# MLP up products and attention input projections as seven block products instead of eight

## The chip, the cores and the metric

The kernel runs on one core of one Trainium2 chip. The metric is the device time of one execution in microseconds (us). TensorE is called PE (PEld its weight loads), VectorE DVE, ScalarE ACT, GpSimd POOL, SyncE SP; SP issues most of the DMAs.

## The reference

An encoder trunk of two layers over 1024 tokens of width 1024, in fp32. Each layer is `h = h + mixer(rmsnorm(h) * g)` and then `h = h + square(relu(rmsnorm(h) * g @ w1)) @ w2`, with `w1` 1024x4096 and `w2` 4096x1024. The mixer of layer 0 is a retention with four heads (input projection 1024x6144, output 2048x1024), that of layer 1 a chunked attention with sixteen heads (input projection `h @ w_in`, 1024x3072 for q, k and v; output 1024x1024). A last RMSNorm follows.

## The kernel before

All activations are kept feature-major: `h[m]` holds 128 features of all 1024 tokens. An fp32 product is made of three matmuls on reduced-precision parts: each operand is split into `hi` (a cast, on ACT) and `lo` (source minus `hi`, on DVE or POOL), and `mm3` (L162 to L164) adds hi·hi, lo·hi and hi·lo in PSUM. Each matmul has 128 rows of contraction, 128 output features and 512 tokens (a half, `hf`).

An up product (`proj_up`, `up_group`) takes 128 columns of `w1`, loads them (`wraw`, 512 KB, on SP), splits them (`whi`, `wlo`), and does 8 blocks x 3 = 24 matmuls for each half. The operands `hhi`, `hlo` are made with the gain `g` in `Norm.block`, which `down` calls as soon as a block of `h` is final, so during the last products of the stage before; the scale per token, `rB`, comes from `Norm.finish` behind the first products. In `mlp` four such blocks give 512 features of the hidden layer; relu and scale (DVE, L324), square (ACT) and a split (`uh`, `ul`) leave them in SBUF, and `down` at once multiplies them with 512 rows of `w2` and adds into `h` (DVE, L280). So up and down alternate eight times per MLP, 192 matmuls each. `qk_proj` does the q and k blocks of the attention in the same way and writes them to memory, `proj_tok` makes v token-major. The attention core then loads q and k (`qh`, `kk`), the bias (`bt`) and v (`vst`) per head; the last `qk_proj` is placed behind the loads of the first heads.

Each engine executes its queue in order. The order of the queues comes from a scheduler over the program order; pools of tiles, with a side of SBUF (left, right) and a number of buffers, decide what may overlap.

## Time and profile before

| | |
|---|---|
| median of 3 runs | 2914.6 us (2913.02 to 2916.2) |
| profiled execution | 2915.2 us, its span 2913.1 us |
| PE busy | 2853.9 us, 98% |
| DVE, ACT, POOL busy | 1318.6, 879.7, 395.5 us |
| mean granted PE clock | 0.991 |

The span runs from the first to the last instruction; 2.1 us of the execution lie around it. Matmuls are pipelined, so what one costs is read from the distance of two starts, not from its duration.

### The profile page before, as it was taken

Reading aid. Unit: us, or ns where it says so; the run is one execution under the profiler, and the core shown is the slowest. Engines: PE = TensorE matmul, PEld = TensorE weight load, DVE = VectorE, ACT = ScalarE, POOL = GpSimd, SP = SyncE. Lnnn points to the kernel's source line nnn. Section 1 sums busy time; section 2 is a strip of 40 time slices with the busy share of each in tenths; the row PEclk is TensorE's granted clock in tenths of the full one; section 3 lists DMA queues with packets and bytes.
Section 4 is the critical chain, followed back from the end, with each engine's and each line's share of the span. In section 5 each row is a group of like instructions: output and inputs, shape, how many; then the busy total and the mean of one; then the engine's idle time right before and its main releaser. Section 6 shows DMA issues by size and latency. Waiting matters only on the chain.

```text
span 2913.1 us, 33150 instructions
## 1 busy us (share of the span) xinstructions
PE 2853.9 (98%) x13178; PEld 2360.5 (81%) x13178; DVE 1318.6 (45%) x2194; ACT 879.7 (30%) x1484; POOL 395.5 (14%) x391
## 2 busy tenths in 40 slices
PE   8999999889999999999999999989999999999998
PEld 7888888777787888888888888879987888888887
DVE  6431123455656333333334623388886333333335
ACT  4012122333324222221123313288873221122212
POOL 4320000122213000000000200055551000000002
PEclk9999999999999999999999999999999999999999
DMA  4322233433211111111111464575521111111112
GB/s 131 111 93 99 88 123 98 152 109 109 75 48 38 50 51 44 51 46 49 51 44 51 123 175 168 150 183 154 152 55 50 45 51 44 51 49 46 51 44 72
DMA packets 244041, 245.79 MB, mean 84 GB/s; under 512 B 10968, under 2 KB 195360, under 8 KB 241840
## 3 DMA queue, kind: packets, MB, share of 16 engines
q1 hardware_dynamic: 242400, 240.75, 27.8%
q10 hardware_dynamic: 1488, 2.95, 0.4%
q8 instruction: 103, 1.69, 0.2%
q14 instruction: 50, 0.41, 0.1%
HBM read 189.09 MB, written 57.19 MB: 85 GB/s over the span
## 4 chain that ended last, share of the span: by engine, by line
PE 89%; DVE 5%; ACT 3%; POOL 1%; DMA 1%; issue 1%; SPq 0%; POOLq 0%; ACTq 0%; DVEq 0%
PE ps L163 28%; PE ps L162 28%; PE ps L164 28%; PE po L888 1%; PE pt L876 1%; ACT pr L856 1%; ACT pth L137 1%; PE pS L847 1%; DVE hlo L190 1%; PE pS L848 1%; DVE pr L852 0%; POOL acc L200 0%; DMA xt<-in_x_dram 0%; DVE ptl L141 0%; PE pt L629 0%
## 5 line engine op out<-in xcount | busy, mean ns | idle before, releaser
L162 PE MATMUL ps<-hhi,whi 128*128 128x512 f32 x1792 | 698.8, 390 | 3.7 <-DVE rc L394 2.4
L163 PE MATMUL ps<-hlo,whi 128*128 128x512 f32 x1792 | 698.8, 390 | 1.4 <-DVE hlo L190 1.4
L164 PE MATMUL ps<-hhi,wlo 128*128 128x512 f32 x1792 | 698.8, 390 | 0.8 <-DVE wlo L141 0.8
L137 ACT CAST whi<-wraw 128x1024 fp32r<-128x1024 f32 x220 | 231.7, 1053 | 1256.4 <-PE ps L163 1027.4
L280 DVE TENSOR_TENSOR h<-ps,h 128x512 f32<-128x512 f32 x368 | 253.5, 689 | 464.4 <-PE ps L164 461.8
L162 PEld LDWEIGHTS ps<-hhi,whi 128*128 128x128 f32 x1792 | 337.2, 188 | 74.9 <-DVE rc L394 2.8
L163 PEld LDWEIGHTS ps<-hlo,whi 128*128 128x128 f32 x1792 | 337.0, 188 | 72.3 <-DVE hlo L190 2.1
L164 PEld LDWEIGHTS ps<-hhi,wlo 128*128 128x128 f32 x1792 | 337.1, 188 | 71.4 <-DVE wlo L141 1.2
L162 PE MATMUL ps<-uh,whi 128*128 128x512 f32 x960 | 379.7, 396 | 0.0
L163 PE MATMUL ps<-ul,whi 128*128 128x512 f32 x960 | 379.7, 396 | 0.0
L164 PE MATMUL ps<-uh,wlo 128*128 128x512 f32 x960 | 379.7, 396 | 0.0
L141 DVE TENSOR_TENSOR wlo<-wraw,whi 128x1024 fp32r<-128x1024 f32 x213 | 266.8, 1252 | 237.2 <-ACT whi L137 237.1
L200 POOL TENSOR_TENSOR acc<-acc,sq 128x512 f32<-128x512 f32 x70 | 102.4, 1464 | 1419.7 <-ACT sq L199 1413.9
L324 DVE SCALAR_TENSOR_TENSOR t<-ps,rB 128x512 f32<-128x512 f32 x128 | 88.0, 691 | 320.7 <-PE ps L164 320.7
L163 PEld LDWEIGHTS ps<-ul,whi 128*128 128x128 f32 x960 | 180.3, 188 | 43.6
L162 PEld LDWEIGHTS ps<-uh,whi 128*128 128x128 f32 x960 | 180.3, 188 | 43.6
L164 PEld LDWEIGHTS ps<-uh,wlo 128*128 128x128 f32 x960 | 180.3, 188 | 43.6
L325 ACT ACTIVATE t<-t 128x512 f32<-128x512 f32 x128 | 80.5, 630 | 262.1 <-DVE t L324 262.1
L162 PE MATMUL ps<-whi,hhi 128*128 128x512 f32 x384 | 149.4, 389 | 0.1
L164 PE MATMUL ps<-whi,hlo 128*128 128x512 f32 x384 | 149.4, 389 | 0.0
L163 PE MATMUL ps<-wlo,hhi 128*128 128x512 f32 x384 | 149.4, 389 | 0.0
L141 DVE TENSOR_TENSOR ul<-t,uh 128x512 fp32r<-128x512 f32 x128 | 88.3, 692 | 80.6 <-ACT uh L137 80.6
(185 smaller groups left out, 3657.5 us busy)
## 6 DMA issues: line engine op xcount, KB each, us to landing
wraw<-in_mlp_w_dram SPq DMA_DIRECT2D x128, 512.0 KB, 3.8
wraw<-in_ret_w_in_dram SPq DMA_DIRECT2D x48, 512.0 KB, 4.0
kk<-kA SPq DMA_DIRECT2D x32, 512.0 KB, 8.1
wraw<-in_att_w_in_dram SPq DMA_DIRECT2D x24, 512.0 KB, 4.0
vS<-t SPq DMA_DIRECT2D x32, 256.0 KB, 2.0
gS<-t SPq DMA_DIRECT2D x32, 256.0 KB, 2.0
wraw<-in_ret_w_out_dram SPq DMA_DIRECT2D x16, 512.0 KB, 3.5
raw<-vS SPq DMA_DIRECT2D x16, 512.0 KB, 4.6
```

The lines of the kernel that those rows point to most:

```text
L137: nc.scalar.copy(out=hi, in_=src)
L141: eng.tensor_tensor(out=lo, in0=src, in1=hi.bitcast(F32), op=ALU.subtract)
L162: nc.tensor.matmul(ps, lhsT=lh, rhs=rh, start=start, stop=False)
L163: nc.tensor.matmul(ps, lhsT=lh, rhs=rl, start=False, stop=False)
L164: nc.tensor.matmul(ps, lhsT=ll, rhs=rh, start=False, stop=stop)
L190: nc.vector.scalar_tensor_tensor(out=lo, in0=src, scalar=g, in1=hi.bitcast(F32), op0=ALU.mult, op1=ALU.subtract)
L200: nc.gpsimd.tensor_tensor(out=self.acc[hf], in0=self.acc[hf], in1=sq, op=ALU.add)
L280: nc.vector.tensor_tensor(out=hv, in0=ps, in1=hv, op=ALU.add)
L324: nc.vector.scalar_tensor_tensor(out=t, in0=res[hf], scalar=0.0, in1=rB[:, hf * HT:(hf + 1) * HT], op0=ALU.max, op1=ALU.mult)
L325: nc.scalar.activation(t, t, AF.Square)
L847: nc.tensor.matmul(ps[:, y, :hw], lhsT=qs, rhs=kh[:, ks], start=True, stop=False)
L848: nc.tensor.matmul(ps[:, y, :hw], lhsT=qs, rhs=kl[:, ks], start=False, stop=True)
```

## The change

Strassen's form (Winograd's variant) is used for the up products of both MLPs and for q, k and v of the attention. The width of 1024 is cut into even and odd blocks of 128, the tokens into the two halves, and the columns into pairs of 128 (a `Group`: 256 columns, one load `wr` of 1 MB). Seven products of 4 blocks x 3 = 12 matmuls, in the order 1, 2, 6, 5, 7, 3, 4, give the four results that took 4 x 24 matmuls. Per group four sums of weight blocks (`wS`) are made on POOL and seven weights split (`wh` on ACT, `wl` on DVE); three banks A, B, C of PSUM hold running sums, which are copied (`s1`, `s6`, `s5`, ACT) and added (DVE). On the other side seven combinations of the operands are needed: 1, 2, 6, 5 are made in `XNorm.block` during the stage before, 7, 3 and 4 in `late`, called at the start of the stage. `fin` (the scale `rB`) is a hook in the first group.

An MLP now does all its up products first (`mlp_up`, 16 groups) and writes the hidden layer to memory (`uD`, 256 KB per result); `mlp_down` reads it back (`ur`, 1 MB per half chunk, one buffer) and splits it. v is made feature-major and turned by four transposes per result. All loads of the attention core now follow the last projection. The pool of the plain weights moves from the left side of SBUF to the right, into one pool per stage.

```diff
+    def tmp_tile(pl, name, dt=F32):
+        return pl.tile([P, HT], dt, name=name, tag="tmp", bufs=8 if pl is plain.get("gp") else 5)
...
+    EARLY, LATE = (1, 2, 6, 5), (7, 3, 4)
+    SEVEN = EARLY + LATE
+    class Operands:
+        def __init__(self):
+            self.hi, self.lo = {}, {}
+        def add(self, pl, products):
+            for p in products:
+                self.hi[p] = pl.tile([P, 4, HT], F32R, name=f"xh{p}", tag=f"xh{p}")
+                self.lo[p] = pl.tile([P, 4, HT], F32R, name=f"xl{p}", tag=f"xl{p}")
+        def split(self, p, j, raw):
+            split(raw, self.hi[p][:, j, :], self.lo[p][:, j, :])
+    class XNorm(Norm):
+        def __init__(self, gain, gp, xa, xt, bufs):
+            super().__init__(gain, gp, False)
+            self.fresh = lambda: xt.tile([P, HT], F32, name="xr", tag="xr", bufs=bufs)
+            self.x = Operands()
+            self.x.add(xa, EARLY)
+            self.seen = {}
+        def own(self, name, dt=F32):
+            return tmp_tile(self.gp, name, dt)
+        def parts(self, j):
+            g = [gains[:, self.gain, 2 * j + z:2 * j + z + 1] for z in range(2)]
+            b = [[h[2 * j + z][:, hf * HT:(hf + 1) * HT] for hf in range(2)] for z in range(2)]
+            return g, b
+        def block(self, m, hf):
+            self.square(m, hf)
+            j = m // 2
+            self.seen[j] = self.seen.get(j, 0) + 1
+            if self.seen[j] < 4:
+                return
+            x, (g, b) = self.x, self.parts(j)
+            b11, b21, t1, t2 = (self.fresh() for _ in range(4))
+            nc.scalar.activation(b11, b[0][0], AF.Copy, scale=g[0])
+            nc.scalar.activation(b21, b[1][0], AF.Copy, scale=g[1])
+            x.split(1, j, b11)
+            x.split(2, j, b21)
+            nc.vector.scalar_tensor_tensor(out=t1, in0=b[0][1], scalar=g[0], in1=b11, op0=ALU.mult, op1=ALU.subtract)
+            nc.vector.scalar_tensor_tensor(out=t2, in0=b[1][1], scalar=g[1], in1=t1, op0=ALU.mult, op1=ALU.subtract)
+            x.split(6, j, t2)
+            x.split(5, j, t1)
+        def late(self, xb):
+            x, gp = self.x, self.gp
+            x.add(xb, LATE)
+            for j in range(4):
+                g, b = self.parts(j)
+                b22, t3 = tmp_tile(gp, "b22"), tmp_tile(gp, "t3")
+                nc.scalar.activation(b22, b[1][1], AF.Copy, scale=g[1])
+                nc.vector.scalar_tensor_tensor(out=t3, in0=b[0][1], scalar=g[0], in1=b22, op0=ALU.mult, op1=ALU.subtract)
+                x.split(7, j, t3)
+                x.split(3, j, b22)
+            for j in range(4):
+                g, b = self.parts(j)
+                t4 = tmp_tile(gp, "t4")
+                nc.vector.scalar_tensor_tensor(out=t4, in0=b[1][0], scalar=g[1], in1=x.hi[6][:, j, :].bitcast(F32), op0=ALU.mult, op1=ALU.subtract)
+                nc.gpsimd.tensor_tensor(out=t4, in0=t4, in1=x.lo[6][:, j, :].bitcast(F32), op=ALU.subtract)
+                x.split(4, j, t4)
+    class Group:
+        def __init__(self, ws, src):
+            self.ws, self.w = ws, {}
+            raw = ws.tile([P, NB, 2 * P], F32, name="wr", tag="wr", bufs=2)
+            DMA.dma_start(out=raw, in_=src.rearrange("(k p) c -> p k c", p=P))
+            self.a = {(f, k): raw[:, k::2, f * P:(f + 1) * P] for f in range(2) for k in range(2)}
+            self.s = {}
+        def sums(self, products):
+            a = self.a
+            for p in products:
+                self.s[p] = t = self.ws.tile([P, 4, P], F32, name="wS", tag="wS", bufs=3)
+                if p == 5:
+                    nc.gpsimd.tensor_tensor(out=t, in0=a[1, 0], in1=a[1, 1], op=ALU.add)
+                elif p == 6:
+                    nc.gpsimd.tensor_tensor(out=t, in0=self.s[5], in1=a[0, 0], op=ALU.subtract)
+                elif p == 7:
+                    nc.gpsimd.tensor_tensor(out=t, in0=a[1, 0], in1=a[0, 0], op=ALU.subtract)
+                else:
+                    nc.gpsimd.tensor_tensor(out=t, in0=a[0, 1], in1=self.s[6], op=ALU.subtract)
+        def make(self, p):
+            hi = self.ws.tile([P, 4, P], F32R, name="wh", tag="wh", bufs=3)
+            lo = self.ws.tile([P, 4, P], F32R, name="wl", tag="wl", bufs=3)
+            split(self.s[p] if p in self.s else self.a[{1: (0, 0), 2: (0, 1), 4: (1, 1)}[p]], hi, lo)
+            self.w[p] = (hi, lo)
+    def seven(ws, psp, gp, x, jobs, hooks=None):
+        groups, steps = {}, [(i, p) for i in range(len(jobs)) for p in SEVEN]
+        AHEAD = 2
+        def ready(s):
+            if s >= len(steps):
+                return
+            i, p = steps[s]
+            if p == 1:
+                if i == 0:
+                    groups[0] = Group(ws, jobs[0][0])
+                if i + 1 < len(jobs):
+                    groups[i + 1] = Group(ws, jobs[i + 1][0])
+                if i == 0:
+                    groups[0].sums((5, 6))
+            elif p == 2 and i == 0:
+                groups[0].sums((3, 7))
+            if p == 4 and i + 1 < len(jobs):
+                groups[i + 1].sums((5, 6))
+            if p == 2 and i:
+                groups[i].sums((3, 7))
+            groups[i].make(p)
+        for s in range(AHEAD):
+            ready(s)
+        held = {}
+        for s, (i, p) in enumerate(steps):
+            ready(s + AHEAD)
+            done = jobs[i][1]
+            if p in (1, 2, 5):
+                held[{1: "A", 2: "B", 5: "C"}[p]] = psp.tile([P, HT], F32, name="pABC"[0:1] + {1: "A", 2: "B", 5: "C"}[p],
+                                                         tag={1: "A", 2: "B", 5: "C"}[p], bufs=2)
+            bank = held[{1: "A", 6: "A", 7: "A", 4: "A", 2: "B", 5: "C", 3: "C"}[p]]
+            wh, wl = groups[i].w.pop(p)
+            for j in range(4):
+                mm3(bank, (wh[:, j, :], wl[:, j, :]), (x.hi[p][:, j, :], x.lo[p][:, j, :]), p in (1, 2, 5) and j == 0, j == 3, p in (6, 7, 4, 3))
+            if p in (1, 6, 5):
+                held[p] = t = tmp_tile(gp, f"s{p}")
+                nc.scalar.copy(out=t, in_=bank)
+            elif p == 4:
+                done(1, 0, bank)
+                groups.pop(i)
+            else:
+                t = tmp_tile(gp, "c")
+                nc.vector.tensor_tensor(out=t, in0=bank, in1=held[{2: 1, 7: 5, 3: 6}[p]], op=ALU.add)
+                done(*{2: (0, 0), 7: (1, 1), 3: (0, 1)}[p], t)
+            if hooks and (i, p) in hooks:
+                hooks[i, p]()
...
+    def mlp_up(norm, w1, uS):
+        gp = norm.gp
+        with ExitStack() as st:
+            xb = pool(st, "xlate", LEFT)
+            ws = pool(st, "wseven", LEFT)
+            psp = pool(st, "psU", None, 2, PSUM)
+            norm.late(xb)
+            def job(g):
+                def done(z, hf, src):
+                    t = tmp_tile(gp, "c") if z == 1 and hf == 0 else src
+                    nc.vector.scalar_tensor_tensor(out=t, in0=src, scalar=0.0, in1=rB[:, hf * HT:(hf + 1) * HT], op0=ALU.max, op1=ALU.mult)
+                    nc.scalar.activation(t, t, AF.Square)
+                    DMA.dma_start(out=uS[g // 2][hf, 2 * (g % 2) + z], in_=t)
+                return w1[:, g * 2 * P:(g + 1) * 2 * P], done
+            def fin():
+                for hf in range(2):
+                    norm.finish(psp, hf)
+            seven(ws, psp, gp, norm.x, [job(g) for g in range(DFF // (2 * P))], {(0, 1): fin})
+    def mlp_down(psp, up, uS, w2, norm, last=None):
+        U = {}
+        def splits(c):
+            for hf in range(2):
+                raw = up.tile([P, 4, HT], F32, name="ur", tag="ur", bufs=1)
+                DMA.dma_start(out=raw, in_=uS[c][hf].rearrange("b p t -> p b t"))
+                for b in range(4):
+                    a = up.tile([P, HT], F32R, name="uh", tag="uh", bufs=11)
+                    z = up.tile([P, HT], F32R, name="ul", tag="ul", bufs=11)
+                    split(raw[:, b, :], a, z)
+                    U[c, b, hf] = (a, z)
+                    yield
+        run(splits(0))
         for c in range(NB):
-            uh, ul = [], []
-            for b in range(4):
-                res = proj_up(psp, norm, w1[:, (4 * c + b) * P:(4 * c + b + 1) * P])
...
-            if c == NB - 1:
-                if last is not None:
-                    return last(w2[c * 512:(c + 1) * 512, :], lambda kb, hf: (uh[2 * kb + hf], ul[2 * kb + hf]))
-                nxt = mk_norm()
-            run(down(dict(psp=psp, norm=nxt), w2[c * 512:(c + 1) * 512, :], 4, lambda kb, hf: (uh[2 * kb + hf], ul[2 * kb + hf])))
-        return nxt
+            nxt = splits(c + 1) if c + 1 < NB else None
+            src = w2[c * 512:(c + 1) * 512, :]
+            rhs = lambda kb, hf, c=c: U[c, kb, hf]
+            if c == NB - 1 and last is not None:
+                return last(src, rhs)
+            for i, _ in enumerate(down(dict(psp=psp, norm=norm if c == NB - 1 else None), src, 4, rhs)):
+                if nxt and i >= 8:
+                    next(nxt, None)
+            if nxt:
+                run(nxt)
...
             psp = pool(st, "psB", None, 8, PSUM)
-            norm = Norm(2, gp)
+            xt = pool(st, "xraw", RIGHT)
+            norm = XNorm(2, gp, xa, xt, 10)
             box.update(psp=psp, norm=norm)
             run(tail)
         rs.close()
+    mlp_up(norm, I["mlp_w1"][0], uD)
+    xs.close()
+    xs = ctx.enter_context(ExitStack())
+    xa = pool(xs, "xearlyD", LEFT)
     with ExitStack() as ph:
+        plain["wp"] = pool(ph, "weightsC", RIGHT)
+        up = pool(ph, "upC", RIGHT)
         psp = pool(ph, "psC", None, 8, PSUM)
-        up = pool(ph, "upC", RIGHT)
-        norm = mlp(psp, up, norm, I["mlp_w1"][0], I["mlp_w2"][0], lambda: Norm(1, gp))
+        norm = XNorm(1, gp, xa, up, 4)
+        mlp_down(psp, up, uD, I["mlp_w2"][0], norm)
...
+        def v_job(i):
+            def done(z, hf, src):
+                b = 2 * i + z
+                t = tmp_tile(gp, "c") if z == 1 and hf == 0 else src
+                nc.vector.tensor_tensor(out=t, in0=src, in1=rB[:, hf * HT:(hf + 1) * HT], op=ALU.mult)
+                pv = psp.tile([P, 4, 2, DH], F32, name="pv", tag="ps")
+                for y in range(4):
+                    nc.tensor.transpose(pv[:, y, :, :].rearrange("p a f -> p (a f)"), t[:, y * P:(y + 1) * P], ident)
+                for y in range(2):
+                    vt = tmp_tile(gp, "vt", F32R).rearrange("p (t q f) -> p t q f", t=2, q=4)
+                    hi, lo, part = vt[:, :, 0:4:3, :], vt[:, :, 1:3, :], pv[:, 2 * y:2 * y + 2, :, :]
+                    nc.scalar.copy(out=hi, in_=part)
+                    nc.vector.tensor_tensor(out=lo, in0=part, in1=hi.bitcast(F32), op=ALU.subtract)
+                    r0 = hf * HT + 2 * y * P
+                    DMA.dma_start(out=vA[b // 4][r0:r0 + 2 * P, (b % 4) * 2 * P:(b % 4 + 1) * 2 * P].rearrange("(t p) c -> p t c", p=P),
+                                  in_=vt.rearrange("p t q f -> p t (q f)").bitcast(F32))
+            c0 = 2 * D + i * 2 * P
+            return w_in[:, c0:c0 + 2 * P], done
+        def fin():
+            for hf in range(2):
+                norm.finish(psp, hf)
...
+        jobs = [qk_job(0, 0), qk_job(1, 0)] + [v_job(i) for i in range(4)]
+        for i in range(1, 4):
+            jobs += [qk_job(0, i), qk_job(1, i)]
+        seven(ws, psp, gp, norm.x, jobs, {(0, 1): fin, (2, 1): bias_rows})
+    xs.close()
+    gs.close()
+    with ExitStack() as ph:
+        rs = ctx.enter_context(ExitStack())
         op_ = pool(rs, "oA", RIGHT)
+        plain["wp"] = pool(rs, "weightsA", RIGHT)
+        rq = ctx.enter_context(ExitStack())
         cq = pool(rq, "coreAqk", RIGHT)
...
-        qk_proj(NP - 1)
```

DVE at the start of the first MLP before the change: the last blocks of the retention output are added into `h` (L280), the operands of the MLP (`hlo`) follow each, and the split of the first weights (L141 `wlo`) stands between them; `ah`, `al` and `vv` belong to `Norm.finish`.

```order
590 L190 SCALAR_TENSOR_TENSOR hlo<-h_91,gall,hhi 128x512
591 L139 CAST ah<-acc_6210 128x512
592 L280 TENSOR_TENSOR h_90<-ps,h_90 128x512
593 L141 TENSOR_TENSOR al<-acc_6210,ah 128x512
594 L190 SCALAR_TENSOR_TENSOR hlo<-h_90,gall,hhi 128x512
595 L280 TENSOR_TENSOR h_91<-ps,h_91 128x512
596 L141 TENSOR_TENSOR wlo<-wraw,whi 128x1024
597 L190 SCALAR_TENSOR_TENSOR hlo<-h_91,gall,hhi 128x512
598 L139 CAST ah<-acc_6211 128x512
599 L225 TENSOR_SCALAR vv<-pss 128x512
600 L141 TENSOR_TENSOR al<-acc_6211,ah 128x512
601 L141 TENSOR_TENSOR wlo<-wraw,whi 128x1024
```

The same place after the change, behind the last add into `h`: `t` and `b` are combinations of the operands (L306 and L312 make them, L140 splits them into `xl`); number 6570 is product 7, 6572 product 3, 6574 product 4, and `wl<-wr` is the split of the weights of products 1 and 2.

```order
609 L140 TENSOR_TENSOR xl_6572<-b_6591,xh_6571 128x512
610 L306 SCALAR_TENSOR_TENSOR t_6600<-h_87,gall,b_6599 128x512
611 L140 TENSOR_TENSOR xl_6572<-b_6599,xh_6571 128x512
612 L312 SCALAR_TENSOR_TENSOR t_6607<-h_82,gall,xh_6230 128x512
613 L140 TENSOR_TENSOR xl_6570<-t_6600,xh_6569 128x512
614 L312 SCALAR_TENSOR_TENSOR t_6612<-h_84,gall,xh_6230 128x512
615 L140 TENSOR_TENSOR xl_6574<-t_6607,xh_6573 128x512
616 L312 SCALAR_TENSOR_TENSOR t_6617<-h_86,gall,xh_6230 128x512
617 L140 TENSOR_TENSOR xl_6574<-t_6612,xh_6573 128x512
618 L312 SCALAR_TENSOR_TENSOR t_6622<-h_88,gall,xh_6230 128x512
619 L140 TENSOR_TENSOR xl_6574<-t_6617,xh_6573 128x512
620 L140 TENSOR_TENSOR wl<-wr,wh 128x512 x2
```

The split of the first weights now stands behind the combinations of the late products.

SP at a passage from up to down before the change (loads of `w1` blocks, then of `w2` units, four each):

```order
159 L619 DMA gt<-gS_107 128x4x256
160 L146 DMA wraw<-in_mlp_w_dram 128x8x128 x4
161 L146 DMA wraw<-in_mlp_w_dram 128x4x256 x4
162 L146 DMA wraw<-in_mlp_w_dram 128x8x128 x4
163 L146 DMA wraw<-in_mlp_w_dram 128x4x256 x4
```

After it, at the end of the first `mlp_up`:

```order
196 L495 DMA uD_112<-c 128x512 x7
197 L511 DMA ur<-uD_105 128x4x512
198 L495 DMA uD_112<-c 128x512
199 L147 DMA wraw<-in_mlp_w_dram 128x4x256 x2
200 L511 DMA ur<-uD_105 128x4x512
201 L147 DMA wraw<-in_mlp_w_dram 128x4x256 x2
```

The first two loads of `w2` now stand behind the write of the last result of the up products and the first read of the hidden layer.

SP at the loads of the first attention head before the change (`kA` and `qA` with L733 are writes of projections):

```order
225 L767 DMA qh<-qA_10910 128x1024
226 L733 DMA kA_10920<-dhi 64x512 x2
227 L733 DMA kA_10920<-t 64x512 x2
228 L146 DMA wraw<-in_att_w_in_dram 128x2x512
229 L773 DMA kk<-kA_10918 64x2048
```

After the change:

```order
350 L933 DMA kA_11483<-c 64x512
351 L933 DMA kA_11483<-dhi 64x512
352 L933 DMA kA_11483<-c 64x512
353 L993 DMA qh<-qA_11468 128x1024
354 L999 DMA kk<-kA_11476 64x2048 x2
```

They stood among the writes of later projections, and now stand behind the last of them.

## Rows read from the trace of the kernel before

**Rows 1.** The page: span, busy time and share of each engine.

```profile
span 2913.1 us, 33150 instructions
PE 2853.9 (98%) x13178; PEld 2360.5 (81%) x13178; DVE 1318.6 (45%) x2194; ACT 879.7 (30%) x1484; POOL 395.5 (14%) x391
```

**Rows 2.** The page: the chain that ended last, by engine.

```profile
PE 89%; DVE 5%; ACT 3%; POOL 1%; DMA 1%; issue 1%; SPq 0%; POOLq 0%; ACTq 0%; DVEq 0%
```

**Rows 3.** Timeline of PE, up and down products: start, duration, instruction.

```profile
1039.82 0.39 PE L163 MATMUL ps<-hlo,whi 128*128 128x512 f32 x1
...
1052.29 0.39 PE L164 MATMUL ps<-hhi,wlo 128*128 128x512 f32 x1
1052.52 0.40 PE L162 MATMUL ps<-uh,whi 128*128 128x512 f32 x1
...
1063.95 0.40 PE L163 MATMUL ps<-ul,whi 128*128 128x512 f32 x1
```

**Rows 4.** Windows: bounds, length, busy us PE, PEld, DVE, ACT, POOL, clock, DMA, GB/s.

```profile
870.00:930.00 60.00, 57.20 (x242) 45.41 (x241) 35.29 (x47) 26.49 (x43) 24.29 (x18) 0.97 0.13 36
960.00:1060.00 100.00, 100.00 (x437) 81.56 (x436) 36.42 (x46) 21.18 (x29) 0.00 (x0) 1.00 0.16 48
1885.00:1925.00 40.00, 34.18 (x204) 29.45 (x203) 27.89 (x81) 27.47 (x67) 18.09 (x29) 0.91 0.76 197
```

**Rows 5.** Timeline of PE, end of the retention output, after a wait.

```profile
877.05 0.96 PE L162 MATMUL ps<-yh,whi 128*128 128x512 f32 x3 [1.50 <-ACT yh L137]
879.55 0.63 PE L164 MATMUL ps<-yh,wlo 128*128 128x512 f32 x1
882.11 0.42 PE L164 MATMUL ps<-yh,wlo 128*128 128x512 f32 x1
```

**Rows 6.** Groups of DVE: x count, busy us, mean ns of one, idle before.

```profile
L141 DVE TENSOR_TENSOR wlo<-wraw,whi 128x1024 fp32r<-128x1024 f32 x213 | 266.8, 1252 | 237.2 <-ACT whi L137 237.1
L141 DVE TENSOR_TENSOR ul<-t,uh 128x512 fp32r<-128x512 f32 x128 | 88.3, 692 | 80.6 <-ACT uh L137 80.6
L190 DVE SCALAR_TENSOR_TENSOR hlo<-ps,gall,hhi 128x512 fp32r<-128x512 f32 x16 | 11.7, 745 | 7.7 <-ACT hhi L189 7.5
L172 DVE RECIPROCAL rB<-sd 128x512 f32<-128x512 f32 x8 | 26.6, 3340 | 0.2 <-issue 0.2
```

**Rows 7.** Groups of ACT.

```profile
L137 ACT CAST uh<-t 128x512 fp32r<-128x512 f32 x128 | 79.4, 622 | 3.9
L137 ACT CAST whi<-wraw 128x1024 fp32r<-128x1024 f32 x220 | 231.7, 1053 | 1256.4 <-PE ps L163 1027.4 <-PE ps L164 169.7 <-issue 51.5
L171 ACT ACTIVATE sd<-vv 128x512 f32<-128x512 f32 x8 | 5.1, 633 | 11.1 <-DVE vv L225 7.0 <-DVE rcol L172 4.0
L171 ACT ACT_TABLE_LOAD x2 | 2.6, 1283 | 0.6 <-DVE vv L225 0.6
```

**Rows 8.** Groups of POOL.

```profile
L200 POOL TENSOR_TENSOR acc<-acc,sq 128x512 f32<-128x512 f32 x70 | 102.4, 1464 | 1419.7 <-ACT sq L199 1413.9 <-issue 4.3
```

**Rows 9.** Timeline of POOL and of DVE, same place.

```profile
876.39 2.52 POOL L141 TENSOR_TENSOR yl<-yt,yh 128x512 fp32r<-128x512 f32 x2 [4.39 <-ACT yh L137]
877.65 3.52 DVE L190 SCALAR_TENSOR_TENSOR hlo<-h,gall,hhi 128x512 fp32r<-128x512 f32 x2 [1.31 <-ACT hhi L189]
```

**Rows 10.** DMA issues: x count, KB each, median us to landing.

```profile
wraw<-in_mlp_w_dram SPq DMA_DIRECT2D x128, 512.0 KB, 3.8
kk<-kA SPq DMA_DIRECT2D x32, 512.0 KB, 8.1
kA<-t SPq DMA_DIRECT2D x32, 128.0 KB, 2.4
```

**Rows 11.** Waits of PE, whole span: total us, times, longest.

```profile
PE ps L163 <- DVE hlo L190: 1.4, 1, 1.4
PE pS L847 <- DVE sm L852: 4.8, 4, 3.6
```

**Rows 12.** Timeline of PE: eight transposes of 128x128.

```profile
874.22 1.33 PE L629 MATMUL pt<-ident,on 128*128 128x128 f32 x8 [0.34 <-ACT on L607]
```

More of the change, by code (lines that the diff above doesn't have):

```diff
@@ L94, in trunk_kernel @@
     cpool = pool(ctx, "consts", LEFT)
-    wp = pool(ctx, "weights", LEFT)
     hp = pool(ctx, "resid", LEFT)
@@ L735, in trunk_kernel @@
-        for p in range(NP // 2):
-            qk_proj(p)
-        with ExitStack() as st:
-            vw = pool(st, "ext", RIGHT)
-            ext = vw.tile([AH, 640], F32, name="ext")
-            nc.vector.memset(ext, 0.0)
-            nc.scalar.dma_start(out=ext[:, 319:639], in_=I["att_rel_bias"][0])
-            nc.vector.tensor_scalar(out=ext[:, 319:639], in0=ext[:, 319:639], scalar1=-1.0, scalar2=None, op0=ALU.mult)
-            nc.vector.tensor_scalar(out=ext[:, 0:319], in0=ext[:, 0:319], scalar1=ext[:, 319:320], scalar2=None, op0=ALU.add)
-            nc.scalar.dma_start(out=extd, in_=ext)
+        xb = pool(ph, "xlateD", LEFT)
@@ new lines, in trunk_kernel, with qk_job @@
+        ws = pool(ph, "wsevenD", LEFT)
+        psp = pool(ph, "psD", None, 2, PSUM)
+        norm.late(xb)
+        def qk_job(which, i):
+            def done(z, hf, src):
+                p, dst = 2 * i + z, (qA, kA)[which]
+                sl = slice(hf * HT, (hf + 1) * HT)
+                t = tmp_tile(gp, "c") if z == 1 and hf == 0 else src
+                if which == 0:
+                    nc.vector.scalar_tensor_tensor(out=t, in0=src, scalar=-ATT_SCALE, in1=rB[:, sl], op0=ALU.mult, op1=ALU.mult)
+                else:
+                    nc.vector.tensor_tensor(out=t, in0=src, in1=rB[:, sl], op=ALU.mult)
+                hi = tmp_tile(gp, "dhi", F32R)
+                nc.scalar.copy(out=hi, in_=t)
+                nc.vector.tensor_tensor(out=t, in0=t, in1=hi.bitcast(F32), op=ALU.subtract)
+                for a in range(2):
+                    rows = slice(a * DH, (a + 1) * DH)
+                    for y, part in ((0, hi.bitcast(F32)), (1, t)):
+                        DMA.dma_start(out=dst[p][a, y, :, sl] if which == 0 else dst[p][a, :, y, sl], in_=part[rows, :])
+            c0 = which * D + i * 2 * P
+            return w_in[:, c0:c0 + 2 * P], done
```

122 lines of the change are left out of this document (48 added, 74 removed).

## The prediction

> **What bounds the kernel now.** I read the page first: PE is busy for 2853.9 of 2913.1 us [rows 1], and 89% of the chain that ended last is PE's [rows 2]. So almost every microsecond is a matmul that waits only for the one ahead of it. Then the windows, since a mean over stages hides where other engines count. Inside the first MLP (960 to 1060 us) PE is busy all the time, DVE 36%, ACT 21% and POOL not at all [rows 4]: there, only PE's time counts, and the others have room. Then the timeline of PE for the price of one matmul, from start to start: the 55 steps from 1039.82 to 1052.29 us (up) give 12.47 / 55 = 0.2267 us, the 49 from 1052.52 to 1063.95 (down) 11.43 / 49 = 0.2333 us [rows 3]. Last, the places where stages meet, since the change puts new work there. Now they cost little: from 870 to 930 us PE misses 2.8 us [rows 4], of which 1.4 is the one wait for an operand of the MLP [rows 11] and 1.5 stands at 877.05 ahead of the last retention products [rows 5]. The start of the attention core misses 5.8 us in 40, at a clock of 0.91 [rows 4]; its longest wait, 3.6 us, is for the first softmax [rows 11].
>
> **What the change removes.** Two MLPs have 16 groups each, q, k and v 12: 44 groups with 84 matmuls for 96, 528 fewer. At 0.2267 us that is **-119.7 us**, and all of it is on the path.
>
> **Inside the groups** PE needs 84 x 0.2267 = 19.0 us. In an MLP group DVE has seven splits, three adds and four relu-scales of 128x512, 14 x 0.69 [rows 6] = 9.7 us; ACT seven casts, three copies, four squares, 14 x 0.62 [rows 7] = 8.7 us; POOL four sums at 1.46 [rows 8] = 5.9 us. All stay below 19.0, so in the steady state nothing is lost: weights are made two products (5.4 us) ahead, and the tightest step, a copy out of a bank of PSUM ahead of its next product, has 1.4 us to spare by these durations. A q or k group has 18 operations on DVE, 12.4 us; if all of POOL's 5.9 us were taken from DVE, 18.3 of 19.0. I take **+3 us** for the eight such groups together, between 0 and 16 (2 us each).
>
> DVE and POOL do get in each other's way. Two `hlo` on DVE took 3.52 us, 1.76 each, while POOL made `yl` [rows 9]; the same operation from PSUM takes 0.745 [rows 6]. The Trainium skill, page "SBUF — State Buffer", section "SBUF: two separate sides", says that an operation of VectorE with two SBUF inputs and one of GpSimd exclude each other for a whole instruction. Rows 9 agree (1.0 us more for each). By this rule the ten DVE operations of an MLP group with two SBUF inputs could lose some 2 us per group when they meet a busy POOL, which the 9 us of room hold: the same sum, an estimate of mine from that page and these rows.
>
> **Starts of the up stages (three).** Let E be the end of the last product ahead. The load of the first weights (1 MB) waits for the memory that this product reads, and takes some 7.6 us (twice the 3.8 of half the size [rows 10]). But in DVE's queue the split of product 1's weights is the 23rd operation counted from the last add into `h`: nine with a gain at 0.745 and fourteen at 0.69 [rows 6] make 16.4 us, and one split is ahead of them (0.7). Eight POOL operations lie in this stretch (the last square's sum, three weight sums, four steps of product 4's operand); between nothing and 1.0 us for each [rows 9] I take 3, and 1 for the way of product 4's operand from DVE over POOL and ACT back to DVE. So PE, after four matmuls, goes on at E + 21 (17 to 25). It then runs at half clock as after the wait at 877 us, where six steps from 879.55 to 882.11 took 0.427 each [rows 5]: the rest of product 1 takes 3.9 us. Product 2 with the row sums 3.6; products 6 and 5 with a wait of 1.0 for `al` 6.4; then the copy `s6` stands on ACT behind the second square root (table 1.28 and 0.63 [rows 7]), 2.1; product 7 2.7; the weights of product 3 stand on DVE behind the second reciprocal (3.34 [rows 6]), 2.6; products 3 and 4 with 0.8 for an add 6.2. The first group ends at E + 48.5; its matmuls and the row sums are worth 20. Less the 1.4 us of wait that stood there before: **+27 us**, for the first MLP and the attention projections alike. At the second MLP the stage ahead has only six matmuls per result: 96 x 0.2333 = 22.4 us of PE against some 40 DVE operations (28 us) and 14 sums on POOL (20.5 us), so DVE is 6 us late at E already. There the split of product 1's weights stands earlier (E + 12), but product 2's is 18 operations later (E + 27), and both reciprocals with six operations behind them are ahead of product 3's weights (E + 46); the group ends at E + 52: **+31 us**. Together 85, with bounds of 60 (no loss to POOL and the scale hidden) and 102.
>
> **Up to down (twice).** The first load of `w2` stands on SP behind the write of the last result, which needs DVE and ACT (0.69 + 0.62); then 3.8 for the load [rows 10], 1.05 for the cast [rows 7] and 1.25 for `wlo` [rows 6]: 7.4 us, and 1.6 for eight matmuls at half clock [rows 5]. The hidden layer's first read starts 5 us before E and is covered by this. **+18 us** for both (14 to 24). Later reads (2 MB per 45 us of products) are covered by the chunk ahead.
>
> **Start of the attention core.** The loads of the first head stand behind the last writes of k, which need DVE, ACT, DVE (2.0 us) and four more writes (2.4 us each to land [rows 10]); `kk` lands 8.1 us after its issue [rows 10]. Before, it was covered by the last q and k projection. **+12 us** (8 to 16); the wait for the softmax stays.
>
> **Transposes for v:** 64 at 1.33 / 8 = 0.17 us [rows 12] with short waits for their source: **+10** (7 to 18).
>
> **Sum:** -119.7 + 85 + 18 + 12 + 10 + 3 = +8.3 us. The profiled execution took 2915.2 us (0.6 above the median of 2914.6, less than the spread of the three runs): **2923.5 us**. With all the bounds at once, -31 to +56.
>
> **Rivals.**
> *The starts are hidden (faster).* If the combinations of products 7, 3 and 4 don't hold up PE, a start costs the load (7.6) and the scale's waits (6), 14 for 28: 2882 us. For it: the hook with the scale is behind product 1, DVE is only 35 of 60 us busy at 870 to 930 us [rows 4]. Against it: the queue's order, which the engine can't leave.
> *POOL holds up every group (slower).* If a blocked DVE operation (1.0 us [rows 9]) reaches a copy out of PSUM past its room of 1.4 us in most groups, say 0.7 us each, 44 groups add 31: 2954. For it: rows 9, and POOL was idle in this stage before [rows 4]. It decides from 1.4 us of delay on. The rule of the Trainium skill's page "SBUF — State Buffer" is the one by which it would come.
> *The rate of the matmuls changes.* Up and down differ by 0.0066 us per matmul [rows 3], and the trace doesn't say why; the moving operand of down lies on the right side of SBUF, its weights on the left. If having both on one side is what makes 0.2267, the 4224 matmuls of down and of both output projections gain 28 us, since their weights move right, and 2304 of the retention's projections lose 15: 2910. If the products of the new form run at 0.2333, 3696 x 0.0066 = 24 more: 2948.
> That the change doesn't do what it says can be left out: the matmuls are fewer by count.
>
> **How the numbers follow.** The sum as forecast has 0.48 (its own range 2905 to 2942), hidden starts 0.27, POOL in every group 0.15, the rate 0.10. No change that can be told is within 0.2%, 2908.8 to 2920.4. Faster: hidden starts 0.27, 0.04 of the rate, 0.03 of the forecast's lower end, 0.34. Within: 0.12 of the forecast, 0.05 of the rate, 0.17. Slower: the rest, 0.49. The range of 2885 to 2955 leaves out the ends where all bounds meet.
>
> **What would show it.** In the profile after: some 12,700 matmuls; steps of 0.2267 us in the up stages with PE busy all the time from the second group on; three stretches of some 50 us behind a last add into `h` in which PE is busy for 20, waiting for `wl` on DVE and then for `s6` on ACT; two waits of some 7 us for `whi` or `wlo` behind a DMA; one of some 12 us for `kk`. Wrong it would be most of all if the starts are shorter (PE waits for `wl` under 12 us), or if PE's share inside the groups falls below 98%, or if the steps in down are no longer 0.2333.

## The result and the profile after

The changed kernel took 2947.7 us (median of four runs, 2945.8 to 2948.6) against 2915.0 for the kernel before beside it: a ratio of 1.0112, with a 95% interval of 1.0094 to 1.0129. It is slower, by 33 us. The profiled execution has a span of 2943.9 us, 30.8 more than before [rows 1].

The page of the changed kernel, its span, the engines and the chain that ended last:

```profile
span 2943.9 us, 34310 instructions
PE 2754.1 (94%) x12698; PEld 2275.5 (77%) x12698; DVE 1565.9 (53%) x2637; ACT 1070.1 (36%) x1906; POOL 661.3 (22%) x579
PE 83%; DVE 8%; ACT 3%; DMA 2%; POOL 2%; issue 1%; SPq 0%; ACTq 0%; POOLq 0%; DVEq 0%
```

PE is busy for 99.8 us less [rows 1], and the span is longer all the same: PE's idle time went from 59.2 to 189.8 us. The chain names who holds it now. DVE, DMA and POOL have grown against [rows 2]. The longest of PE's waits say for what (total us, times, longest):

```profile
PE pA L164 <- ACT wh L136: 28.2, 2, 15.9
PE pA L166 <- DVE wl L140: 23.8, 3, 11.2
PE ps L164 <- ACT whi L136: 20.8, 3, 9.6
PE pA L164 <- ACT s L385: 16.5, 4, 7.3
PE pS L1070 <- DMA kk<-kA: 15.7, 1, 15.7
PE pA L164 <- DVE xl L140: 13.4, 1, 13.4
```

Before, the one wait for an operand of an MLP was 1.4 [rows 11]. The new ones come few times and long, so they are at the meeting points of stages and not in every group. The windows around the first MLP's start say the same (columns as in [rows 4]; E, the end of the last product ahead, is at 926.27):

```profile
926.00:938.00 12.00, 0.27 (x2) 0.00 (x0) 10.63 (x11) 7.58 (x14) 6.47 (x5) 0.72 0.54 175
938.00:952.00 14.00, 2.26 (x4) 1.00 (x4) 13.60 (x16) 5.12 (x10) 6.99 (x4) 0.50 0.00 0
952.00:985.00 33.00, 28.87 (x115) 22.25 (x116) 26.57 (x34) 11.08 (x20) 8.43 (x6) 0.95 0.19 64
985.00:1255.00 270.00, 270.00 (x1193) 223.62 (x1192) 128.33 (x199) 116.43 (x199) 75.47 (x55) 1.00 0.32 107
```

For 26 us after E PE does next to nothing, DVE is busy for 24.2 of them, and the granted clock falls to its lower level (0.50 in the second row). From 985 us on PE is busy for 270 us out of 270: inside the groups nothing is lost.

The lengths of the stages, from PE's timelines of both kernels (us, from the end of one stage's last product to that of the next; the first from the start of its first product):

```
stage                              before    after   difference
retention projections (to 1st core) 538.8    552.0      +13.2
retention core and output           367.4    361.1       -6.3
first MLP                           708.4    698.7       -9.7
q, k, v projections                 265.0    283.4      +18.4
attention core, its start, output   290.5    304.0      +13.5
second MLP                          714.6    714.8       +0.2
end                                  15.5     16.7       +1.2
```

An MLP drops 192 matmuls, worth 43.5 us, and is shorter by 9.7 at most. The projections drop 144, worth 32.6, and their stage and the next are 32 longer. And the retention projections, in which the number of matmuls is the same, take 13 more. The timeline of PE shows why for these: 48 steps of the retention's projections and 48 of down, in the changed kernel.

```profile
300.15 0.40 PE L166 MATMUL ps<-whi,hlo 128*128 128x512 f32 x1
...
311.35 0.40 PE L166 MATMUL ps<-whi,hlo 128*128 128x512 f32 x1
...
1450.09 0.39 PE L164 MATMUL ps<-uh,whi 128*128 128x512 f32 x1
...
1460.97 0.39 PE L164 MATMUL ps<-uh,whi 128*128 128x512 f32 x1
```

11.20 / 48 = 0.2333 and 10.88 / 48 = 0.2267. The two have changed places against the kernel before, where down had 0.2333 [rows 3], and 48 steps of the retention's projections took 10.88 us, 0.2267 each:

```profile
295.88 0.39 PE L162 MATMUL ps<-whi,hhi 128*128 128x512 f32 x1
...
306.76 0.39 PE L162 MATMUL ps<-whi,hhi 128*128 128x512 f32 x1
```

So 10.2 us of what an MLP became shorter come from the 1536 steps of its down products. The 43.5 us of its up products are used up.

### The profile page after: what moved, and what is told of

Same layout as the page of the kernel before. It is cut to its first block, busy times and chain, and to the rows that moved or that the text cites. A ratio compares the mean times of both kernels' runs of the same rounds, so it can differ in the third digit from the quotient of the medians.

```text
span 2943.9 us, 34310 instructions
## 1 busy us (share of the span) xinstructions
PE 2754.1 (94%) x12698; PEld 2275.5 (77%) x12698; DVE 1565.9 (53%) x2637; ACT 1070.1 (36%) x1906; POOL 661.3 (22%) x579
## 4 chain that ended last, share of the span: by engine, by line
PE 83%; DVE 8%; ACT 3%; DMA 2%; POOL 2%; issue 1%; SPq 0%; ACTq 0%; POOLq 0%; DVEq 0%
PE ps L164 17%; PE ps L166 17%; PE ps L165 17%; PE pA L166 5%; PE pA L164 5%; PE pA L165 5%; PE pC L164 3%; PE pC L166 3%; PE pC L165 3%; DVE xl L140 1%; PE po L1111 1%; PE pB L166 1%; PE pB L165 1%; PE pB L164 1%; PE pt L1099 1%
## 5 line engine op out<-in xcount | busy, mean ns | idle before, releaser
L164 PE MATMUL pA<-xh,wh 128*128 128x512 f32 x704 | 279.5, 397 | 59.1 <-ACT wh L136 28.2
L166 PE MATMUL pA<-xh,wl 128*128 128x512 f32 x704 | 278.0, 395 | 23.8 <-DVE wl L140 23.8
L165 PE MATMUL pA<-xl,wh 128*128 128x512 f32 x704 | 277.9, 395 | 0.0
L140 DVE TENSOR_TENSOR wlo<-wraw,whi 128x1024 fp32r<-128x1024 f32 x125 | 159.8, 1278 | 169.7 <-ACT whi L136 169.4
L164 PE MATMUL ps<-hhi,whi 128*128 128x512 f32 x512 | 203.3, 397 | 4.3 <-ACT whi L136 1.8
L164 PEld LDWEIGHTS pA<-xh,wh 128*128 128x128 f32 x704 | 134.5, 191 | 90.4 <-ACT wh L136 43.4
L166 PE MATMUL ps<-hhi,wlo 128*128 128x512 f32 x512 | 203.0, 396 | 1.2 <-DVE wlo L140 1.2
L165 PE MATMUL ps<-hlo,whi 128*128 128x512 f32 x512 | 202.9, 396 | 0.0
L140 DVE TENSOR_TENSOR wl<-wS,wh 128x512 fp32r<-128x512 f32 x176 | 123.2, 700 | 109.1 <-ACT wh L136 108.7
L166 PEld LDWEIGHTS pA<-xh,wl 128*128 128x128 f32 x704 | 134.1, 190 | 53.8 <-DVE wl L140 26.0
L165 PEld LDWEIGHTS pA<-xl,wh 128*128 128x128 f32 x704 | 134.5, 191 | 27.5
```

The source lines that it names most:

```text
L140: eng.tensor_tensor(out=lo, in0=src, in1=hi.bitcast(F32), op=ALU.subtract)
L164: nc.tensor.matmul(ps, lhsT=lh, rhs=rh, start=start, stop=False, skip_group_check=more)
L165: nc.tensor.matmul(ps, lhsT=lh, rhs=rl, start=False, stop=False, skip_group_check=more)
L166: nc.tensor.matmul(ps, lhsT=ll, rhs=rh, start=False, stop=stop, skip_group_check=more)
```

## The experiments

Two questions were open: what makes a matmul take 0.2267 or 0.2333 us, and which of the things at the start of a stage holds PE up.

### What sets a matmul's step

**Base of the right side moved by 32 bytes, kernel before and kernel after.** Only the place of everything on SBUF's right side changes.

```diff
+    pad = pool(ctx, "pad", RIGHT).tile([P, 8], F32, name="pad")
+    nc.vector.memset(pad, 0.0)
```

> The kernel before with a tile of 32 bytes at the base of the right side of SBUF, nothing else. Theory A, the step between matmuls depends on how the addresses of the two operands stand to each other below 64 bytes: in down and both output projections (4224 matmuls) the moving operand then stands like the weights, 0.2333 becomes 0.2267 us: -28, 2887 us. Theory B, the side itself or something else makes the difference: unchanged, 2915.

> The changed kernel with the same 32 bytes. Theory A: only the retention's input projections (2304 matmuls, operands left, weights right) are mismatched there, they go back from 0.2333 to 0.2267: -15, 2932 us. Theory B: unchanged, 2948.

Measured: 2914.7 us, ratio 0.9997 (0.9987 to 1.0006), for the kernel before, and 2944.2 us, 1.0094 (1.0077 to 1.0111), for the one after. Neither moved beyond its interval: agreement modulo 64 is not the condition. A part of the second kernel's steps did change, in the first of the retention's projections (86 to 201 us):

```profile
107.98 0.39 PE L169 MATMUL ps<-hhi,wlo 128*128 128x512 f32 x1
...
118.97 0.39 PE L169 MATMUL ps<-hhi,wlo 128*128 128x512 f32 x1
```

10.99 / 48 = 0.229, a value between the two.

**480, 96 and 224 bytes, kernel before.** The same lines with 120, 24 and 56 elements. By the sizes of the pools, 480 bytes bring the two sides to equal addresses modulo 512, 224 modulo 256 and 96 modulo 128 alone; this is worked out from the program, a trace shows no addresses.

> The kernel before with 480 bytes at the base of the right side, so that every tile there stands like the weights on the left modulo 512 bytes (the step from one block of weights to the next). Theory A2, the place of the two operands modulo up to 512 bytes sets the step between matmuls: 4224 matmuls of down and the output projections go from 0.2333 to 0.2267, -28: 2887 us. Theory B, both operands on one side of SBUF is what counts: unchanged, 2915.

> The kernel before with 96 bytes at the base of the right side: its right side then stands at the left side's addresses modulo 128, not modulo 256 or 512. If 128 is what the matmul step depends on: down and output products at 0.2267 and 2892, ratio 0.992. If it is 256 or 512: unchanged at 2915, the down products at 0.2333.

> The kernel before with 224 bytes at the base of the right side, which leaves the right side at the left side's addresses modulo 256 but not modulo 512. If 256 is what the matmul step depends on: down at 0.2267 and 2892, ratio 0.992. If it is 512: unchanged at 2915, the down products at 0.2333.

Measured: 2892.1 us, 0.9921 (0.9906 to 0.9936), with 480; 2914.7, 0.9999 (0.9990 to 1.0008), with 96; 2887.8, 0.9914 (0.9899 to 0.9929), with 224. Down in the timelines of PE, 48 steps each, with 96 bytes:

```profile
1049.71 0.40 PE L165 MATMUL ps<-uh,whi 128*128 128x512 f32 x1
...
1060.91 0.40 PE L165 MATMUL ps<-uh,whi 128*128 128x512 f32 x1
```

and with 224 bytes:

```profile
1043.23 0.39 PE L165 MATMUL ps<-uh,whi 128*128 128x512 f32 x1
...
1054.11 0.39 PE L165 MATMUL ps<-uh,whi 128*128 128x512 f32 x1
```

0.2333 with 96 bytes and 0.2267 with 224 (with 480 as well), while both operands stay on opposite sides. So the side itself is not the cause. What fits all runs is the distance of the two operands' addresses: the short step where it is a multiple of 256 bytes, a longer one elsewhere (0.2333, and in parts of two runs 0.229 with 32 bytes and 0.232 with 96). A threshold between 96 and 224 bytes instead of a remainder is not excluded by these pads alone. The changed kernel's own down speaks against it: no pad, both operands on the right, and 0.2267. Why the step depends on it stays open, and so does whether 224 bytes beat 480, whose intervals overlap.

### What holds a stage's start

**The weights of the first two products ahead of the late operands.** The operands of products 7, 3 and 4 are issued behind the first two weight splits.

```diff
-            norm.late(xb)
...
         for s in range(AHEAD):
             ready(s)
+        if then:
+            then()
```

> The changed kernel, but in the program the weights of products 1 and 2 of the first group come ahead of the combinations of products 7, 3 and 4. Theory 1, a start is long because DVE's queue has these combinations ahead of the first weights: products 1 and 2 begin some 10 us earlier in the first MLP and the attention projections, part of which is given back where products 7, 3 and 4 wait: -15 to -30, about 2925. Rival, the 1 MB load of weights that waits for the end of the stage before sets the start: unchanged, 2948.

Measured: 2942.8 us, 1.0094 (1.0079 to 1.0109), some 5 us less; the interval overlaps that of the changed kernel. The first wait at the first MLP falls from 12.3 to 6.9 us, since ACT's queue too had the late operands ahead of the first weights. Their cast, first in the changed kernel, then here:

```profile
937.95 0.60 ACT L136 CAST wh<-wr 128x512 fp32r<-128x512 f32 x1
...
932.78 1.13 ACT L136 CAST wh<-wr 128x512 fp32r<-128x512 f32 x2
```

The wait of 11.2 for `wl` falls to 3.6, but there are now eight waits, 6.9, 3.6, 3.5, 1.3, 0.6, 2.1, 1.9 and 0.9 us: the loss went to the products behind. At the other two starts the first wait is nearly as before (13.5 for 13.4, 15.3 for 15.9). The order alone is not the cause.

**No late operands.** The 40 operations at each start are left out, and products 7, 3 and 4 take the operands of 5, 2 and 6.

```diff
+            for p, q in ((7, 5), (3, 2), (4, 6)):
+                x.hi[p], x.lo[p] = x.hi[q], x.lo[q]
+            return
```

> The changed kernel without the combinations of products 7, 3 and 4: these use the operands of products 5, 2 and 6 instead, so 12 splits and 8 or more further operations on DVE and 4 on POOL are left out at each of the three starts. Theory 1: each start loses some 15 us: 2903. Rival (load and scale set the start): less than 5 each, above 2933.

Measured: 2892.0 us, 0.9919 (0.9899 to 0.9939), 56 us less. The up stage of the first MLP goes from 337.6 to 320.7 us, that of the second from 349.5 to 334.5, and the stage of the projections with the start of the core is 22 shorter. The first two are what the making of these operands, which no PE work covers, costs there: 17.0 and 15.0 us. The 22 are not that alone. In this kernel the first loads of the core came out in the middle of the projections in SP's queue:

```profile
1680.57 0.47 SPq L1002 DMA_DIRECT2D kk<-kA  x1
```

So PE's wait of 15.7 us for `kk` is gone as well, while a wait for `s` in the projections has grown from 6.1 to 16.0. How much of the 22 belongs to the operands, this run doesn't show.

**Nothing on POOL at a start.** Product 4's second subtraction and the first group's weight sums go to DVE.

```diff
-                nc.gpsimd.tensor_tensor(out=t4, in0=t4, in1=x.lo[6][:, j, :].bitcast(F32), op=ALU.subtract)
+                nc.vector.tensor_tensor(out=t4, in0=t4, in1=x.lo[6][:, j, :].bitcast(F32), op=ALU.subtract)
...
-                    groups[0].sums((5, 6))
+                    groups[0].sums((5, 6), nc.vector)
```

> The changed kernel with product 4's subtraction and the weight sums of the first group on DVE instead of POOL (eight operations at each start, the same arithmetic). Theory 2, at the starts DVE and POOL exclude each other, so POOL's slow operations hold the queue that PE waits for: 5 to 8 us less per start, 2924 to 2933. Rival, DVE is simply full and now gets more work: 2948 to 2955.

Measured: 2932.6 us, 1.0066 (1.0051 to 1.0081), 15 us less, though DVE has more to do. The timeline of the changed kernel shows what was paid, first DVE, then POOL, over the same microseconds:

```profile
942.74 1.75 DVE L312 SCALAR_TENSOR_TENSOR t<-h,gall,xh 128x512 f32<-128x512 f32 x1
944.63 0.69 DVE L140 TENSOR_TENSOR xl<-t,xh 128x512 fp32r<-128x512 f32 x1
945.24 1.75 DVE L312 SCALAR_TENSOR_TENSOR t<-h,gall,xh 128x512 f32<-128x512 f32 x1
...
950.23 2.35 DVE L140 TENSOR_TENSOR wl<-wr,wh 128x512 fp32r<-128x512 f32 x2
...
942.37 1.58 POOL L313 TENSOR_TENSOR t<-t,xl 128x512 f32<-128x512 f32 x1 [5.63 <-DVE t L312]
944.64 1.80 POOL L313 TENSOR_TENSOR t<-t,xl 128x512 f32<-128x512 f32 x1 [0.69 <-ACT xh L136]
947.13 1.80 POOL L313 TENSOR_TENSOR t<-t,xl 128x512 f32<-128x512 f32 x1 [0.69 <-ACT xh L136]
```

The same three kinds of line with the subtraction on DVE:

```profile
943.72 0.74 DVE L312 SCALAR_TENSOR_TENSOR t<-h,gall,xh 128x512 f32<-128x512 f32 x1
944.38 1.28 DVE L140 TENSOR_TENSOR xl<-t,xh 128x512 fp32r<-128x512 f32 x2
945.59 0.68 DVE L313 TENSOR_TENSOR t<-t,xl 128x512 f32<-128x512 f32 x1
```

L312 takes 1.75 us beside POOL and 0.74 without, and the two engines run in lockstep, one turn per 2.49 us (944.64 to 947.13). So POOL's help costs DVE 1.0 us each time and saves it 0.68. This is the lock of the Trainium skill's page "SBUF — State Buffer", section "SBUF: two separate sides", and the trace agrees with it: the two operations of 1.75 us end 0.54 and 0.55 us behind the end of the POOL operation that had begun before them.

**The late operands spread over eight products.** The first two groups run in the order 1, 2, 6, 5 of both, then 3, 7, 4 of both, so that there is more PE work ahead of the first late operand; these are made in eight parts, one per product; product 4's subtraction is on DVE.

```diff
+        steps = [(i, p) for ps in ((1, 2, 6, 5), (3, 7, 4)) for i in range(2) for p in ps]
+        steps += [(i, p) for i in range(2, len(jobs)) for p in SEVEN]
...
             ready(s + AHEAD)
+            next(late, None)
```

> The changed kernel with the first two groups' products in the order 1, 2, 6, 5 of both and then 3, 7, 4 of both (in that order), the combinations of products 7, 3 and 4 made in eight parts between them, and product 4's subtraction on DVE. Theory 1: 21.8 us of products now cover the late work, each start loses 12 to 20 us: 2890 to 2912. Rival: DVE is full in both cases, the waiting only moves from the first group into the second: above 2930.

Measured: 2931.8 us, 1.0060 (1.0043 to 1.0077), 16 us less, in sum as with POOL's work moved alone, but in other stages: the two up stages are 5.5 and 9.0 us shorter (4.2 and 3.3 there), the projections 0.4 (4.8 there). Now PE starts earlier (7.2 us of wait for the weights, then 2.8), but at 963.80 it waits again, and the windows of this kernel's first 59 us show on whom:

```profile
926.00:942.00 16.00, 6.03 (x15) 4.22 (x15) 11.37 (x12) 5.67 (x10) 7.39 (x6) 0.68 0.42 132
942.00:985.00 43.00, 34.60 (x134) 26.63 (x133) 39.11 (x52) 20.71 (x36) 7.18 (x5) 0.88 0.13 43
```

DVE is busy for 39.1 of 43 us. Its first 60 us hold the operands, the scale with two reciprocals and the first groups' splits, and in both orders tried here PE still waits for what DVE makes. At the second MLP the first wait is nearly unchanged, 15.2 us against 15.9.

**The last writes issued by ScalarE.** The last activations of an MLP and the last k leave through ACT's queue, so that SP's next loads don't stand behind them.

```diff
-                    DMA.dma_start(out=uS[g // 2][hf, 2 * (g % 2) + z], in_=t)
+                    eng = nc.scalar if g == DFF // (2 * P) - 1 else DMA
+                    eng.dma_start(out=uS[g // 2][hf, 2 * (g % 2) + z], in_=t)
...
```

> The changed kernel with the writes of the last up group and of the last k group issued by ACT instead of SP, so that SP's loads for the next stage don't stand behind them. If SP's order holds these loads up: some 2.4 us less at each passage from up to down and 3 to 6 at the core's start, 2937 to 2941. Rival, the memory that the loads need comes free only then, or the landing sets it: unchanged, 2948.

Measured: 2931.0 us, 1.0055 (1.0040 to 1.0070), 17 us less. PE's waits in this kernel, to be held against the third and fifth row of the changed kernel's:

```profile
PE ps L164 <- ACT whi L136: 12.1, 3, 5.3
PE pS L1072 <- DMA bt<-skew: 9.0, 1, 9.0
```

Up to down goes from 9.6 and 9.5 to 5.3 and 5.0 us, the start of the core from 15.7 to 9.0, where the load waited for is now that of the bias (`bt`). The 17 us are more than the 7 to 11 that were expected. The loads did stand in SP's queue behind writes that were waiting for their data.

### The parts together

**The new form in the MLPs alone.** The attention projections as before the change; 480 bytes at the base of the right side in the retention and attention stages; the spread start and the writes on ACT.

```diff
-        norm = XNorm(1, gp, xa, up, 4)
+        norm = Norm(1, gp)
...
+        pad = pool(rs, "padA", RIGHT).tile([P, 120], F32, name="padA")
+        plain["wp"] = pool(rs, "weightsA", RIGHT)
```

> The two MLP up products as seven products with their activations through memory, the attention's projections as before the change, the 480 bytes at the base of the right side in the retention and attention stages, the first two groups' products in the order of the spread start, the last activations issued by ScalarE. If the sums of this study hold: 2892 (the kernel before with 480 bytes) less 2 x 44 of matmuls each MLP saves in its up product (192 of 1536 steps x 0.2267), plus a start of about 22 and a passage of about 5 in each: about 2860 (2850 to 2872), ratio 0.981. If the loss of the change lies in the MLPs and not in the attention projections: 2892 or more. Matmul steps 0.2267 in every stage.

**All of it.** The whole changed kernel with the same three edits, the bytes in the retention stage alone.

> The changed kernel whole (the attention's projections as seven products too), with 480 bytes at the base of the right side in the retention stage, the spread start and the last writes on ScalarE. If the gains of the single runs add: 2948 less 15 (2304 steps of the retention's projections at 0.2267), 16 and 17: 2900 (2892 to 2908), ratio 0.995. That is 17 above the version with the new form in the MLPs alone, if the projections in the new form lose what the stages' lengths say (their stage up to the attention core 292 to 299 us, against 273 in the old form). If the new form pays in the projections once the starts are mended: under 2880.

Measured: 2882.7 us, 0.9888 (0.9872 to 0.9905), for the first, the lowest median of this study, and 2902.2 us, 0.9959 (0.9945 to 0.9974), for the second. That the first beats the kernel before with nothing but 224 bytes (2887.8) is not shown: the two intervals overlap. The second is as the single gains add up (2900). The first is not: 2860 was expected. Its MLPs take 690.3 and 701.0 us against 697.9 and 706.0 in the kernel before with 480 bytes, so 43.5 us fewer matmuls bring 7.6 and 5.0. Its windows from E = 911.92 (a start that is mended as far as these edits go) and of the groups behind it:

```profile
912.00:985.00 73.00, 54.39 (x205) 42.06 (x206) 59.85 (x78) 32.45 (x55) 21.16 (x16) 0.84 0.27 87
985.00:1240.00 255.00, 255.00 (x1126) 211.15 (x1125) 120.31 (x187) 109.47 (x187) 69.75 (x51) 1.00 0.31 105
```

The first up stage ends 332.3 us after E, its 1344 matmuls are worth 304.7: a start still costs 27.6 us, and I had put it at 22. Waits are 18.4 of it (7.5, 2.6, 7.0, 0.9 and 0.4) and the row sums 0.9; the rest, 8.3, is the lower clock, 0.84 over these 73 us. At the second MLP 15.2 us of the first wait stay. And the stage of the projections is 7.8 longer than in the kernel before with 480 bytes, of which 3.6 are a wait for the first weights (`whi`) behind down.

With the new form in the projections as well, the stage up to the core takes 292.9 us against 272.8: 144 matmuls fewer, and 20.1 us more. That is the difference of the two versions (19.5).

## Why the prediction was right or wrong

The kernel is slower, as forecast, and the time lies in the range of 2885 to 2955. The likeliest time, 2923.5, is 24 us short, and the time lies outside the sum's own range (2905 to 2942). That the wider range holds is in part luck: without 12.7 us that came back from the rate of the matmuls it would have been 2960. That the time meets the 2948 of the rival in which the new products run at 0.2333 is chance, since they run at 0.2267. Two things that the forecast called signs of being wrong were seen: steps of down that are no longer 0.2333, and waits for `wl` under 12 us (11.2, 10.3 and 2.4); the second not because the starts are shorter, but because PE waits longer ahead of it. Against the profiled difference of 30.8 us the terms are as follows.

**The matmuls removed, -119.7:** right. 12,698 are recorded, and a step in the up stages is still 0.2267 us.

**Inside the groups, nothing lost:** right. PE is busy for 270 of 270 us, with DVE at 48% and POOL at 28%. The rival "POOL holds up every group" falls with that row. DVE and POOL do block each other, but the room in a group holds it.

**The rate of the matmuls, kept in the forecast and a rival with 0.10:** this is the step that was wrong in kind: the forecast kept every step as it was. Down and both outputs went to 0.2267 and the retention's projections to 0.2333, just those that the rival named, and by its sum 28 - 15 = 13 us were gained. From the stages: 3072 steps of down give 20.5, both outputs 7.6 and 2304 retention projections cost 15.4, 12.7 in all. The reason that I gave with it, both operands on one side, is not the cause, as the pads show; the distance of the addresses fits all runs. The products of the new form, on the left with their weights, stayed at 0.2267.

So the costs came to 30.8 + 119.7 + 12.7 = 163 us where 85 + 10 + 3 + 18 + 12 = 128 were forecast.

**The starts, 85 with transposes 10 and the q and k groups 3, 98 in all:** mis-sized, about 124 measured. At the first MLP the up stage is 32.0 us longer than its products and row sums, 31.3 more than before (27 forecast). The 1.4 us that the forecast took off here were misplaced: PE's waits from 870 to 930 us in the kernel before are 1.5, 1.0 (`yl`) and 0.3, and the wait of 1.4 stands in the second MLP:

```profile
2195.03 0.50 PE L163 MATMUL ps<-hlo,whi 128*128 128x512 f32 x1 [1.38 <-DVE hlo L190]
```

The mechanism is the one described: four matmuls, then DVE. The timeline of PE:

```profile
938.61 0.80 PE L164 MATMUL pA<-xh,wh 128*128 128x512 f32 x1 [12.34 <-ACT wh L136]
...
952.03 0.80 PE L166 MATMUL pA<-xh,wl 128*128 128x512 f32 x1 [11.16 <-DVE wl L140]
952.62 0.63 PE L164 MATMUL pA<-xh,wh 128*128 128x512 f32 x1
953.05 0.63 PE L165 MATMUL pA<-xl,wh 128*128 128x512 f32 x1
...
966.57 0.50 PE L164 MATMUL pA<-xh,wh 128*128 128x512 f32 x1 [1.69 <-ACT s L385]
```

PE goes on at E + 25.8, where 21 (17 to 25) was forecast: I had allowed 3 us for POOL and 1 for the way over three engines, but from 926 to 952 us eight DVE operations beside POOL take about 8 us more than they do alone. The step of 0.43 us behind the wait and the wait for `s` are as forecast. At the second MLP the cost is 43.9, 41.4 more than before (31 forecast): here DVE is late at E, as said, but so is ACT, and the first weights come only after 15.9 us, against 12.3. For the projections the first matmul waits for an operand, `xl` (13.4), then `wl` (10.3), and two waits for `s` (7.3 and 6.1) follow, of which the forecast had none in this size: it had taken the price of the first MLP. At the first of them ACT's queue has the cast of q (`dhi`), which needs the scale, ahead of the copy; at the second it has the issues of the bias rows (`skew`), which are no part of the late operands:

```profile
1710.33 10.08 ACTq L974 DMA_DIRECT2D skew<-extd  x15
1720.45 0.58 ACT L385 COPY s<-pC 128x512 f32<-128x512 f32 x1 [9.74 <-DMA skew<-extd]
```

Beyond their products the projections' stage has 54.9 us (4 before), 37.1 of them these waits, where 40 more were forecast. The 64 transposes take 6.9 of it by PE's timeline, where 10 (7 to 18) were forecast; no wait stands ahead of them. The q and k groups were not measured apart. The rival of hidden starts falls: all three starts are in full view.

**Up to down, 18 for both (14 to 24):** mis-sized, 25 measured. 9.59 and 9.46 us are waits, where 7.4 each was forecast; behind each, some thirteen steps at the lower clock cost 3 us, where 1.6 for eight matmuls was forecast. The place was right: the writes ahead of the load in SP's queue. Moving them to ACT's queue gave back 4.3 and 4.4 us of the waits.

**The start of the core, 12 (8 to 16):** right, 15.7 us for `kk`, at the upper bound, and behind the writes of k, as said.

In sum the direction came from the forecast's own steps. The size was missed by two errors of opposite sign: 13 us of rate that I had set aside, and 35 of costs, some 26 of them at the starts and 7 from up to down.

## What to carry to other kernels

A product with fewer matmuls is worth what its operands' making leaves: add up the vector work that no matmul covers, one start at a time, and set it against what one stage saves; here some 31 and 41 us at a start against 43.5 in an MLP, and 51 against 32.6 in the projections. An operation handed to POOL was no relief here while DVE had operations of two inputs in the same microseconds. Where two stages have steps of different length for the same shape, look at the addresses of both operands before anything else: a few hundred unused bytes gave 22 to 26 us here; the change in its best form added 9 to the one with 480 bytes, and to the other one nothing that is clear of its interval.

## What was not expected of the hardware

A matmul of 128x512 has a step of 0.2267 or 0.2333 us depending on where its two operands lie to each other. For the kernel before, 0, 32 and 96 bytes at the base of the right side gave 0.2333 in down, 224 and 480 gave 0.2267, and the time went from 2915 to 2888 and 2892 us. A distance that is a multiple of 256 bytes, by the sizes of the pools, fits all runs; the mechanism is open.

Shorter waits did not give back their whole length, since PE then worked longer at the lower clock. With the spread start the waits at the first MLP's start fell from 27.5 us (12.3, 11.2, 1.7, 1.4 and 0.9) to 18.3, but the stage's cost over its products went only from 32.0 to 26.5: what is not wait rose from 4.5 to 8.2 us. The granted clock fell once in the changed kernel, for 23.9 us that are mostly wait, and twice with the spread start, for 10.2 us each, each time within a wait (of 7.2 and 7.0) and past its end; PE was busy for 5.5 us of the one stretch and 12.8 of the two (changed kernel, then spread start):

```profile
931.40:955.28 23.88, 5.51 (x12) 3.60 (x13) 22.32 (x25) 9.84 (x18) 13.04 (x8) 0.50 0.11 39
...
931.23:941.45 10.22, 5.34 (x12) 3.76 (x13) 7.50 (x8) 2.88 (x5) 5.80 (x4) 0.50 0.26 92
961.95:972.17 10.22, 7.44 (x17) 5.36 (x18) 10.22 (x15) 4.67 (x8) 1.57 (x1) 0.50 0.07 27
```
